# A norm's modulation on ScalarE or VectorE by a rule, and masked copies behind a condition

## Chip, cores and metric

One of the eight cores of a Trainium2 chip runs the whole kernel in one launch. The metric is the device time of that launch in microseconds. The core has five engines with a queue of their own each: TensorE (PE in the profile; its weight loads are PEld), VectorE (DVE), ScalarE (ACT), GpSimd (POOL) and SyncE (SP), which issues most of the loads.

## What is computed

Two layers over 128 context tokens (b = 0) and 128 latent tokens (b = 1), model width 2048, fp32. Layer 0 is attention, layer 1 a bidirectional state-space mixer (S5); each is followed by a gated MLP with a width-3 convolution (FFN). Each of the four sub-layers starts with a norm and a modulation:

```
h  = rms_norm(x, g) * (1 + scale) + shift          # per channel, from c_ctx or c
x += gate * sublayer(h)
# S5, per direction, 128 groups of 16 channels, 64 complex states:
u   = h @ w_in
s_t = abar * s_{t-1} + B u_t                       # scan over the tokens
y   = gelu(d*u + Re(C s)) ; out = (y * sigmoid(y @ w_gate)) @ w_out
```

A final norm gives y_prompt and y_sample; keys, values and the last scan states are outputs too.

## The kernel before

Each weight unit (128 x 1024 numbers, 512 KB) is loaded into one of eight raw buffers and split for the matmuls: ScalarE rounds it to a high part (whi), VectorE subtracts to get the low part (wlo). There are three whi/wlo buffers, so splits run up to two units ahead. Activations are split in the same way. A product is the sum of three matmuls (high x high, low x high, high x low) into PSUM.

The program is written out by a planner in Python that runs while the kernel is built. `Timeline` holds a clock for each engine (`tl.t`), and every emitted instruction moves its engine's clock by an estimated cost, after what it reads is ready by the same estimate. Side work (norm parameters, attention, FFN's convolution, the S5 scan) is held in generators; `pump()`, called after each weight unit, lets a generator go on when its condition holds by these clocks. `written(ap, lag=...)` is such a condition: the estimated time at which `ap` is written has been passed by TensorE's clock, and neither ScalarE nor VectorE is more than `lag` ahead of it. The order of emission is the order in each engine's queue; on the chip each engine works its queue in that order and waits on semaphores.

`Norm.make` makes the input of one group of k-tiles (four tiles of 128 channels, two in the first two groups of layer 0) for one b. `scale_rows` has VectorE multiply rows of x by 1/rms ahead of time. Then TensorE transposes the tiles into one PSUM bank (`tr`), the modulation multiplies by scale and adds shift per partition, one instruction per tile, ScalarE rounds the result to the high part, VectorE subtracts for the low part. For b = 0 the modulation is on ScalarE, for b = 1 on VectorE. There are ten makes in layer 0's first norm and eight in each of the other three. In the first up block of FFN 0 and FFN 1 and the first block of S5's w_in, three units are computed for b = 0 first and then for b = 1.

S5 works in four quarters q of 512 channels. `w_in` for a quarter ends with two transposes on VectorE that write u(q) and then sets `u_ready[q]`. `scan_task` waits for that flag, copies u(q) twice on ScalarE with a mask per parity (um), has TensorE multiply um by tables (T), and ScalarE writes the products into SC(q). `steps_task` runs the 32 scan steps of a quarter on VectorE, four instructions each. `out_task` copies the states out on ScalarE and has TensorE make y(q), which w_gate then reads. In the trace u, um, h and the split activations are named A, SC is X or S.

All instructions of ScalarE, VectorE and GpSimd, and the DMAs, stand on line 302, matmuls on 404, transposes on 417.

Of the kernel before, what the change touches and what calls it, by code (L numbers as in the profile page):

```python
# [29 lines left out]
S5_LAG = 20  # L30
# [8 lines left out]
Y_TAGS = ('A8', 'A8', 'A2', 'S0')  # L39
GATE_SPLIT = (2, 3)  # L40
SCAN_LAG = 5
TAIL_SPLIT = 1
HEAD_FIRST = 1
T_TAGS = ("A3", "A5", "A3", "A12", "A3", "A8", "A3", "A8")
# [3 lines left out]
def view(t, off, dims, parts=None):  # L48
    p0, pn = (0, t.shape[0]) if parts is None else parts
    ps = t.ap[0][0]  # L50
    return bass.AP(tensor=t.tensor, offset=t.offset + p0 * ps + off,
                   ap=[[ps, pn]] + [list(d) for d in dims])
# [292 lines left out]
def hybrid_kernel(ctx: ExitStack, tc: tile.TileContext, a):  # L345
# [7 lines left out]
    tl = Timeline()  # L353
    TL.append(tl)

    def sb(tag, shape, dt=FT, bufs=1):
        count[0] += 1
        t = pool.tile(list(shape), dt, tag=tag, name=f"{tag}_{count[0]}", bufs=bufs)
        tl.place(t, tag, bufs)
        return t  # L360
# [12 lines left out]
    def ms():  # L373
        return ps("ms", [P, 512], 3)
# [4 lines left out]
    def written(*aps, lag=LAG, ahead=0.1):  # L379

        t = tl.ready(*aps)
        return lambda now: max(t - ahead, tl.t["ACT"] - lag, tl.t["DVE"] - lag) < now

    def ready(*aps, lag=LAG, ahead=0.1):

        t = tl.ready(*aps)
        return lambda now: max(max(t, tl.free("ms", 3)) - ahead, tl.t["ACT"] - lag, tl.t["DVE"] - lag) < now
# [14 lines left out]
    def mm(out, lhsT, rhs, **kw):  # L402
        tl.matmul(out, lhsT, rhs, "tile_position" in kw)
        nc.tensor.matmul(out, lhsT, rhs, **kw)  # L404
# [9 lines left out]
    def tr(out, in_):  # L414
        n = in_.shape[0]
        tl.matmul(out, in_, ident, transpose=True)
        nc.tensor.transpose(out, in_, ident[:n, :n])  # L417
# [211 lines left out]
    def block(w, r0, nkt, n0, ncol, xof, done, head=False, tail=False):  # L629
# [11 lines left out]
        def part(bs, kt0, n, hi, lo):  # L641
            rest = []
            last = kt0 + n == nkt
            for b in bs:
                for kk in range(n):
                    xt, k = xof(kt0 + kk, b)
                    products(cell["acc"], b, xt, k, hi, lo, kk, ncol, kt0 + kk == 0, rest)
            remaining(rest, last, (lambda b: done(cell["acc"], b)) if last else lambda b: None)

        for c0 in range(0, nkt, 4):  # L650
            nk = min(4, nkt - c0)

            def run(k0, n, hi, lo, c0=c0):
# [14 lines left out]
                for i, u in enumerate(cell["kept"] + [me]):  # L668
                    part((1,), *u)
                    if skew == 2 and (head or TAIL_SPLIT <= i < 2):  # L670
                        state["cap"] += 1
# [83 lines left out]
    def ada_need(l, part, kt0, nt=4):  # L755
        for k in range(nt):
            wait_for(ada_tasks[l, part, kt0 + k])
# [24 lines left out]
    class Norm:  # L782
# [25 lines left out]
        def make(self):  # L808
            if self.made == len(self.cells):
                return  # L810
            g, b = self.cells[self.made]
            kt0, nt = self.groups[g]
            l, n = self.l, self.n
            self.scale_rows()
            ada_need(l, 3 * n, kt0, nt)
            ada_need(l, 3 * n + 1, kt0, nt)
            if g not in self.tiles:
                self.tiles[g] = sb(self.tags[g], [P, 2, nt, 256], FR)
            t = self.tiles[g]
            h = self.tmp[0][:, self.made % 4]  # L820
            xn = self.tmp[1][:, self.made % 4, :nt * P]
            ps = ms()
            for k in range(nt):
                tr(ps[:, k * P:(k + 1) * P], xn[:, k * P:(k + 1) * P])
            c = slice(b * P, (b + 1) * P)
            for k in range(nt):
                kt = kt0 + k
                src, dst = ps[:, k * P:(k + 1) * P], h[:, k]
                if self.perm:
                    src = src.rearrange("p (c j) -> p j c", j=4)  # L830
                    dst = dst.rearrange("p (j c) -> p j c", j=4)
                s1, s0 = scale[n][:, kt, b:b + 1], shift[n][:, kt, b:b + 1]
                if b == 0:
                    act(dst, src, AF.Identity, bias=s0, scale=s1)
                else:
                    dve.tensor_scalar(dst, src, s1, s0, op0=OP.mult, op1=OP.add)
            act(t[:, 0, :, c], h[:, :nt], AF.Copy)
            dve.tensor_sub(t[:, 1, :, c], h[:, :nt], t[:, 0, :, c])
            self.made += 1
            self.scale_rows()  # L840
            if self.made == len(self.cells):
                norms.remove(self)
# [683 lines left out]
    class S5:  # L1526
# [64 lines left out]
        def scan_task(self):  # L1591
            while not self.u_ready[0]:
                yield
            wt = self.wt = sb("A11", [P, 2048])
            self.kt = sb("A10", [P, 2048])
            w1 = view(wt, 0, [[64, 2], [32, 2], [1, 32]])
            w2 = view(wt, 128, [[64, 2], [32, 2], [1, 32]])
            for q in range(4):
                while not self.u_ready[q]:
                    yield  # L1600
                while q > 1 and not self.sc_free[q - 2] or q == 1 and not prep[0].done:
                    yield
                um = sb("A2", [P, 16, 2, 2, 32])
                SC = self.SC[q] = sb(("X", "S0")[q % 2], [P, 33, 2, 2, 32])
                u = self.u(q).rearrange("p (r n) -> p r n", n=64)
                for par in range(2):
                    act(um[:, :, par].rearrange("p r b c -> p r (b c)"), u, AF.Copy, scale=mask_par[:, par:par + 1])
                dve.memset(SC[:, 0, :, 0], 0.0)
                dve.tensor_copy(SC[:, 0, :, 1], s5par["H0"][:, :, 32 * q:32 * q + 32])
                for e2 in range(2):  # L1610
                    e = 2 * q + e2
                    while e not in self.tT:
                        yield
                    tT = self.tT[e]
                    for h in range(2):
                        for ri in range(2):
                            yield ready(um, tT[:, h], lag=S5_LAG, ahead=AHEAD)
                            bk = ms()
                            for i in range(4):
                                pr = e2 * 8 + h * 4 + i  # L1620
                                mm(bk[:, i * P:(i + 1) * P], tT[:, h, i, ri],
                                   um[:, pr].rearrange("p a b c -> p (a b c)"), start=True, stop=True)
                            src = bk.rearrange("p (g b c) -> p c b g", b=2, c=32)
                            g0 = e2 * 16 + h * 8
                            fw = view(SC, 128 + ri * 64 + g0, [[128, 32], [32, 2], [1, 8]], (0, 64))
                            bw = view(SC, 32 * 128 + ri * 64 + g0, [[-128, 32], [32, 2], [1, 8]], (64, 64))
                            act(fw, src[0:64], AF.Copy)
                            act(bw, src[64:128], AF.Copy)
                    self.t_used[e] = True
                while self.scanned < q - 1:  # L1630
                    yield
                a_re = view(s5par["A4"], 32 * q, [[0, 2], [0, 2], [1, 32]])
                a_im = view(s5par["A4"], G + 32 * q, [[G, 2], [0, 2], [1, 32]])
                yield written(SC, lag=S5_LAG, ahead=AHEAD)
                self.scans.append((SC, a_re, a_im, w1, w2, q))

        def steps_task(self):
            q = 0
            while q < 4:
# [3 lines left out]
                for s in range(32):  # L1643
# [6 lines left out]
                    dve.tensor_tensor(nxt, nxt, w1, OP.add)  # L1650
                    yield lambda now: tl.t["DVE"] < now + SCAN_LAG
                self.scanned = q
# [316 lines left out]
```

## Time and profile before

| | |
|---|---|
| median of three runs | 2554.88 us (2553.78 to 2556.22) |
| the profiled execution | 2553.2 us, its span 2551.4 us |
| mean granted TensorE clock | 0.993 of full speed |
| TensorE busy | 2481.2 us, 97% |
| VectorE busy | 1669.7 us, 65% |
| ScalarE busy | 1285.4 us, 50% |
| GpSimd busy | 473.1 us, 19% |
| DMA, mean over the span | 256 GB/s |

The span runs from the first to the last instruction of one execution. Busy shares are averages over stages; what an engine waited for stands in brackets behind an instruction, as idle time and releaser. The stages follow each other: layer 0's norm and q, k, v up to about 390 us, attention's output to 520, FFN 0 to 1355, S5 to 1790, FFN 1 to the end.

### The profile page before, as it was taken

Reading aid. Unit: us, or ns where it says so; the run is one execution under the profiler, and the core shown is the slowest. Engines: PE = TensorE matmul, PEld = TensorE weight load, DVE = VectorE, ACT = ScalarE, POOL = GpSimd, SP = SyncE. Lnnn points to the kernel's source line nnn. Section 1 sums busy time; section 2 is a strip of 40 time slices with the busy share of each in tenths; the row PEclk is TensorE's granted clock in tenths of the full one; section 3 lists DMA queues with packets and bytes.
Section 4 is the critical chain, followed back from the end, with each engine's and each line's share of the span. In section 5 each row is a group of like instructions: output and inputs, shape, how many; then the busy total and the mean of one; then the engine's idle time right before and its main releaser. Section 6 shows DMA issues by size and latency. Waiting matters only on the chain. (4 is left out here: it accounts for less than half of the span.)

```text
span 2551.4 us, 37505 instructions
## 1 busy us (share of the span) xinstructions
PE 2481.2 (97%) x13883; PEld 1939.1 (76%) x13883; DVE 1669.7 (65%) x2575; ACT 1285.4 (50%) x1900; POOL 473.1 (19%) x493
## 2 busy tenths in 40 slices
PE   7999999999999999999999989999999999999998
PEld 5676776668887887788776766767688888888886
DVE  3655564578686676676666788454666665766576
ACT  5333354465664564555455554444555544554454
POOL 0002000013565555555511011000000000000000
PEclk9999999999999999999999999999999999999999
DMA  9879978978988888888779677789687766666663
GB/s 359 318 268 295 319 237 301 337 266 258 274 286 264 276 256 261 275 264 271 264 255 322 235 247 246 252 292 317 225 256 242 239 197 185 190 188 196 188 202 124
DMA packets 460495, 653.61 MB, mean 256 GB/s; under 512 B 65420, under 2 KB 245772, under 8 KB 457368
## 3 DMA queue, kind: packets, MB, share of 16 engines
q1 hardware_dynamic: 451744, 620.32, 74.4%
q0 software_dynamic: 8208, 30.35, 3.6%
q8 instruction: 109, 1.79, 0.3%
q14 instruction: 74, 0.61, 0.1%
q10 hardware_dynamic: 360, 0.55, 0.1%
HBM read 623.72 MB, written 27.39 MB: 255 GB/s over the span
## 5 line engine op out<-in xcount | busy, mean ns | idle before, releaser
L302 DVE TENSOR_TENSOR wlo<-raw,whi 128x1024 fp32r<-128x1024 f32 (+1 forms) x694 | 895.2, 1295 | 613.1 <-ACT whi L302 604.8
L302 ACT ACTIVATE whi<-raw 128x1024 fp32r<-128x1024 f32 (+1 forms) x694 | 728.9, 1054 | 597.7 <-PE acc L404 353.4
L404 PE MATMUL acc<-whi,A 128*128 128x512 f32 x3040 | 788.8, 399 | 28.8 <-ACT whi L302 15.4
L404 PEld LDWEIGHTS acc<-whi,A 128*128 128x128 f32 x3040 | 563.2, 189 | 198.3 <-ACT whi L302 33.7
L404 PE MATMUL acc<-A,whi 128*128 128x512 f32 x2496 | 674.2, 395 | 0.0
L404 PEld LDWEIGHTS acc<-A,whi 128*128 128x128 f32 x2496 | 429.9, 189 | 78.4 <-issue 12.2
L404 PE MATMUL acc<-wlo,A 128*128 128x512 f32 x1520 | 415.9, 393 | 0.7 <-DVE wlo L302 0.7
L404 PEld LDWEIGHTS acc<-A,wlo 128*128 128x128 f32 x2496 | 372.3, 190 | 45.7
L404 PE MATMUL acc<-A,wlo 128*128 128x256 f32 x2496 | 383.4, 281 | 0.0
L404 PEld LDWEIGHTS acc<-wlo,A 128*128 128x128 f32 x1520 | 286.8, 189 | 65.2 <-DVE wlo L302 2.4
L302 POOL TENSOR_TENSOR S<-S,A 128x512 f32<-128x512 f32 x128 | 181.7, 1439 | 50.4 <-PE ms L417 50.4
L404 PE MATMUL ada<-raw,cond 128*32 128x512 f32 (+1 forms) x1408 | 169.4, 592 | 1.5 <-DMA raw<-in_ada_w_dram 1.5
L302 POOL DMA_DIRECT2D adab<-in_ada_b_dram x48 | 24.8, 516 | 727.2 <-DVE ada L302 372.6
L302 DVE SCALAR_TENSOR_TENSOR A<-acc,cw,A 128x254 f32<-128x254 f32 x312 | 142.4, 477 | 6.2 <-ACT A L302 0.7
L302 POOL TENSOR_TENSOR S<-S 128x512 f32<-128x512 f32 (+1 forms) x96 | 138.3, 1440 | 7.5
L302 ACT ACTIVATE A<-A 128x512 fp32r<-128x512 f32 (+4 forms) x127 | 81.1, 641 | 113.6 <-DVE A L302 112.5
L302 ACT ACTIVATE A<-acc 128x256 f32<-128x256 f32 (+1 forms) x188 | 69.1, 420 | 110.2 <-PE acc L404 110.1
L302 DVE TENSOR_TENSOR acc<-acc,A 128x256 f32<-128x256 f32 (+1 forms) x228 | 108.9, 508 | 23.6 <-PE acc L404 22.4
L404 PEld LDWEIGHTS ms<-A,A 128*64 128x64 f32 (+1 forms) x1152 | 86.8, 193 | 20.5 <-ACT A L302 8.4
L302 ACT ACTIVATE A<-ms 128x512 f32<-128x512 f32 (+3 forms) x106 | 55.8, 558 | 88.6 <-PE ms L404 69.1
L404 PEld LDWEIGHTS ada<-raw,cond 128*32 128x32 f32 x1408 | 37.9, 109 | 81.3 <-issue 69.8
L404 PE MATMUL ms<-A,A 128*64 128x64 f32 (+1 forms) x1152 | 90.3, 271 | 9.6 <-ACT A L302 5.8
(149 smaller groups left out, 1670.5 us busy)
## 6 DMA issues: line engine op xcount, KB each, us to landing
raw<-in_ada_w_dram SPq DMA_DIRECT2D x334, 512.0 KB
raw<-in_ffn_w_up_dram SPq DMA_DIRECT2D x334, 512.0 KB
raw<-in_ffn_w_down_dram SPq DMA_DIRECT2D x168, 512.0 KB
raw<-in_na_w_qkv_dram SPq DMA_DIRECT2D x68, 512.0 KB
raw<-in_s_w_in_dram SPq DMA_DIRECT2D x32, 512.0 KB
raw<-in_s_w_gate_dram SPq DMA_DIRECT2D x32, 512.0 KB
raw<-in_s_w_out_dram SPq DMA_DIRECT2D x32, 512.0 KB
A<-in_na_w_qkv_dram SPq DMA_DIRECT2D x28, 512.0 KB
```

Source lines behind the costliest of these rows:

```text
L302: return fn(*args, **kw)
L404: nc.tensor.matmul(out, lhsT, rhs, **kw)
```

## The change

A make asks the planner's clocks, once the transposes are emitted, which engine could begin first. If ScalarE, or TensorE where that is later, plus 0.5 us is no later than VectorE, or TensorE where that is later, all of the make's modulations go to ScalarE, otherwise to VectorE; b no longer matters. In `scan_task` the two masked copies are emitted when `written(u, lag=20)` holds instead of as soon as the generator gets there; the memset and the copy of the start state on VectorE follow them, as before.

```diff
+MOD_ACT = 1
...
             c = slice(b * P, (b + 1) * P)
+            by_act = max(tl.t["ACT"], tl.t["PE"]) + 0.5 * MOD_ACT <= max(tl.t["DVE"], tl.t["PE"])
             for k in range(nt):
...
-                if b == 0:
+                if by_act:
                     act(dst, src, AF.Identity, bias=s0, scale=s1)
                 else:
                     dve.tensor_scalar(dst, src, s1, s0, op0=OP.mult, op1=OP.add)
...
                 u = self.u(q).rearrange("p (r n) -> p r n", n=64)
+                yield written(u, lag=S5_LAG)
                 for par in range(2):
                     act(um[:, :, par].rearrange("p r b c -> p r (b c)"), u, AF.Copy, scale=mask_par[:, par:par + 1])
```

## Rows read from the trace of the kernel before

**Rows 1.** The page: busy time, share of the span and instructions of each engine.

```profile
PE 2481.2 (97%) x13883; PEld 1939.1 (76%) x13883; DVE 1669.7 (65%) x2575; ACT 1285.4 (50%) x1900; POOL 473.1 (19%) x493
```

**Rows 2.** TensorE's waits: what it waited for, us in total, times, longest.

```profile
PE acc L404 <- ACT whi L302: 15.4, 9, 3.4
...
PE acc L404 <- ACT A L302: 11.8, 12, 2.4
...
PE ms L417 <- DVE A L302: 7.3, 5, 1.9
```

**Rows 3.** Groups by shape on ScalarE and VectorE: count, busy us, mean ns, idle before.

```profile
L302 ACT ACTIVATE A<-ms,shift,scale 128x128 f32<-128x128 f32 x64 | 24.0, 453 | 21.9 <-PE ms L417 17.0 <-DVE scale L302 5.0
...
L302 DVE TENSOR_SCALAR A<-ms,scale,shift 128x128 f32<-128x128 f32 x64 | 21.8, 401 | 0.0
```

**Rows 4.** Timeline near 114 us: start, us, what, count, idle before and its releaser.

```profile
111.54 0.60 PE L417 MATMUL ms<-ident,A 128*128 128x128 f32 x4
...
114.53 1.36 DVE L302 TENSOR_SCALAR A<-ms,scale,shift 128x128 f32<-128x128 f32 x4
...
115.92 0.63 ACT L302 ACTIVATE A<-A 128x512 fp32r<-128x512 f32 x1 [3.81 <-DVE A L302]
...
116.60 1.00 PE L404 MATMUL acc<-whi,A 128*128 128x512 f32 x2 [2.43 <-ACT A L302]
...
121.98 1.08 PE L404 MATMUL acc<-wlo,A 128*128 128x512 f32 x4
```

**Rows 5.** Timeline near 69 us.

```profile
69.31 0.42 ACT L302 ACTIVATE A<-A 128x256 fp32r<-128x256 f32 x1 [1.93 <-DVE A L302]
...
69.78 0.73 PE L404 MATMUL acc<-whi,A 128*128 128x512 f32 x2 [1.69 <-ACT A L302]
```

**Rows 6.** Timeline of the first makes of FFN 0.

```profile
525.41 1.50 ACT L302 ACTIVATE A<-ms,shift,scale 128x128 f32<-128x128 f32 x4 [0.82 <-PE ms L417]
...
533.15 0.60 PE L417 MATMUL ms<-ident,A 128*128 128x128 f32 x4
...
535.89 0.63 ACT L302 ACTIVATE A<-A 128x512 fp32r<-128x512 f32 x1 [3.13 <-DVE A L302]
...
536.57 0.50 PE L404 MATMUL acc<-whi,A 128*128 128x512 f32 x1 [1.16 <-ACT A L302]
...
545.21 0.63 ACT L302 ACTIVATE A<-A 128x512 fp32r<-128x512 f32 x1 [2.62 <-DVE A L302]
...
545.23 0.66 PE L417 MATMUL ms<-ident,A 128*128 128x128 f32 x4 [1.85 <-DVE A L302]
```

**Rows 7.** Timeline around the masked copies of quarters 0 and 1.

```profile
1396.19 2.19 ACT L302 ACTIVATE A<-A,maskpar 128x1024 f32<-128x1024 f32 x2 [3.47 <-DVE A L302]
...
1430.76 1.30 DVE L302 STREAM_TRANSPOSE A<-acc 128x512 f32<-128x512 f32 x2
...
1432.10 2.19 ACT L302 ACTIVATE A<-A,maskpar 128x1024 f32<-128x1024 f32 x2 [8.30 <-DVE A L302]
...
1435.26 3.50 DVE L302 TENSOR_TENSOR wlo<-raw,whi 128x1024 fp32r<-128x1024 f32 x3 [3.07 <-ACT whi L302]
...
1435.28 3.78 PE L404 MATMUL acc<-whi,A 128*128 128x512 f32 x8 [3.19 <-ACT whi L302]
```

**Rows 8.** Timeline, one undisturbed unit's eight matmuls.

```profile
1408.56 2.09 PE L404 MATMUL acc<-whi,A 128*128 128x512 f32 x8
```

**Rows 9.** Timeline before and after the end of scan 1.

```profile
1483.93 1.23 DVE L302 TENSOR_TENSOR wlo<-raw,whi 128x1024 fp32r<-128x1024 f32 x1 [5.21 <-ACT whi L302]
...
1522.87 8.55 ACT L302 ACTIVATE A<-S 64x1024 f32<-64x1024 f32 x8
...
1525.03 0.50 PE L404 MATMUL ms<-A,A 128*64 128x64 f32 x2 [4.19 <-ACT A L302]
```

**Rows 10.** Stretch: us, busy of PE, PEld, DVE, ACT, POOL, clock, DMA share, GB/s.

```profile
1436.00:1438.00 2.00, 2.00 (x6) 1.52 (x5) 2.00 (x3) 1.12 (x2) 0.00 (x0) 0.50 0.20 31
```

**Rows 11.** Chain that ended last: start, us, what.

```profile
1679.81 10.25 DMA raw<-in_s_w_out_dram
```

## The prediction

> **What bounds the kernel now.** I read the page first: TensorE is busy 2481 of 2551 us [rows 1], so a change can only win what TensorE idles, some 70 us, and the time in which it runs at the lower clock. The list of TensorE's waits then says who holds it: 15.4 us for split copies of weights on ScalarE, 11.8 us for activations written by ScalarE, 7.3 us for ones written by VectorE [rows 2]. These few entries are where both edits act. The groups by shape give the two prices of one modulation, 453 ns on ScalarE and 401 ns on VectorE, 64 of each today [rows 3]: 17 makes with b = 0 go to ScalarE, 17 with b = 1 to VectorE. Last I read the timeline around every stretch in which TensorE stops near a make or near the S5 scan [rows 4 to 11].
>
> **Part one, the modulation.** It removes and adds no instruction; it moves groups of two or four between two engines that each take their work in order. Four take 1.50 us on ScalarE [rows 6] and 1.36 us on VectorE [rows 4], so with both engines free a move to ScalarE costs 0.14 us and the other way gains it. What can be worth more is the work queued in front. In the b = 1 makes VectorE stands behind splits and adds while ScalarE, which must do the next step (the rounded copy), sits idle.
>
> The make near 114 us: the transposes end at 111.54 + 0.60 = 112.14. VectorE starts the modulation at 114.53. ScalarE's copy starts at 115.92 after 3.81 us idle, so it was free from 112.11; TensorE has waited 2.43 us when it goes on at 116.60 [rows 4]. On ScalarE: start 112.2 (0.1 us after the transposes, as elsewhere), plus 1.50, plus the copy 0.63, makes 114.35, 2.2 us earlier. The matmuls behind the stop are slow too: 116.60 to 121.98 is 5.38 us for 16 of them, where eight take 2.09 us in an undisturbed unit [rows 4, 8], so 16 want 4.18: another 1.2 us. Term: 3.4 us.
>
> The make near 69 us (two tiles): ScalarE was free at 69.31 - 1.93 = 67.38 and TensorE waited 1.69 us [rows 5]. Two modulations at about 0.8 and a copy of 0.42 end at 68.65 instead of 69.73. Term: 1.1 us. A like stop of 1.1 us at 25.9 us is left out; loads are tight there.
>
> In each of three norms (FFN 0, S5, FFN 1) the same pair of stops comes twice; I show FFN 0. At 536.57 TensorE has waited 1.16 us: transposes end at 533.75, ScalarE was free from 535.89 - 3.13 = 532.76; on ScalarE the modulation would end at 533.85 + 1.50 = 535.35 instead of 535.86, 0.5 us. At 545.23 TensorE has waited 1.85 us: ScalarE was free at 545.21 - 2.62 = 542.59, would end at 544.1 instead of 545.17, 1.1 us [rows 6]. Three norms: 4.8 us.
>
> Sum of part one: 3.4 + 1.1 + 4.8 = 9.3 us, if the rule picks ScalarE at all these places. It looks at the program's own clocks, which I can't see in a trace; by the queues VectorE is over 1 us behind ScalarE at most of them and about 0.7 us behind the transposes at the three of 0.5 us [rows 4 to 6]. I take seven tenths, 6.5 us, since some picks will fall the other way. Lower end 0; upper end everything and the stop at 25.9 us too: 10.4. The makes near 187 and 273 us have no stop of TensorE beside them and are costed at nothing; the cover is the split copies already made for two units, and without it a make would cost its 1.50 us.
>
> VectorE's own page of the Trainium skill (VectorE: DVE Perf Modes, Specifications) says that ScalarE sits closer to PSUM, by which a modulation that reads PSUM would be quicker there. The trace differs: 453 against 401 ns, 1.50 against 1.36 us for four [rows 3, 4, 6]. The skill's ScalarE: Activation LUTs (What ACT_TABLE_LOAD costs) adds about 93 ns for each per-partition operand, and this instruction has two; that speaks against the move, in the trace's direction. By the first page the sum would be some tenths more, by the second it stays as it is.
>
> **Part two, the masked copies.** It moves two ScalarE instructions of some 1.1 us in each of four quarters behind a condition; SP's and POOL's queues get nothing new. For quarters 2 and 3 the input has been there long before, no effect. For quarter 0 ScalarE idles 3.47 us in front of them but TensorE runs through [rows 7], nothing to win; the price, if the copies and so the products behind them slip by one unit of 12 matmuls, is 2.7 us of a later scan.
>
> Quarter 1 is the place. ScalarE waits 8.30 us at the head of its queue, from 1423.8 to 1432.10, for two transposes that VectorE, busy with scan steps, starts only at 1430.76. Queued behind are the splits of the next units; so VectorE idles 3.07 us (1432.2 to 1435.26) and TensorE 3.19 us (to 1435.28), and its eight matmuls then take 3.78 us, against 2.09 [rows 7, 8]; the granted clock there is 0.50, the lower of its two levels [rows 10]. With the copies emitted a unit or two later the splits pass in front and TensorE saves 3.2 + 1.7 = 4.9 us at this place.
>
> It does not keep them. At 1525.03 TensorE has waited 4.19 us for copies that ScalarE starts at 1522.87, when scan 1 on VectorE has ended [rows 9]. The two scans run back to back on VectorE up to there, so the end moves only by what VectorE gains: its 3.07 us. I take 3.1 us. Lower end -2.7 (quarter 0 slips and VectorE's idle turns up again elsewhere: it stood 5.21 us for a split at 1483.93 [rows 9]); upper end 4.9.
>
> **Sum.** 6.5 + 3.1 = 9.6 us off the profiled 2553.2 us (span 2551.4 and 1.8 around it) is 2543.6. The median of the three runs is 1.7 above the profiled one, so I say 2544.
>
> **Rivals.** (A) The rule seldom fires where TensorE stops, and only part two is left: 2553.2 - 3.1 = 2550. For it: the rule ties to VectorE, and its margin of 0.5 us is as large as the smaller stops. Against it: the idle of ScalarE before the copies is 1.9 to 3.8 us.
>
> (B) TensorE arrives earlier and waits elsewhere: the load that the chain of waits shows at 1679.81 for 10.25 us [rows 11], or the scan. For it: weights are read nearly all the time. Against it: those loads are issued when earlier buffers come free, so they move along. If all of part one before FFN 1 is given back and the scan term too, 1.6 x 0.7 = 1.1 us remains: 2552.
>
> (C) Slower. The rule's tie goes to VectorE, so b = 0 makes leave ScalarE wherever the program believes VectorE free within 0.5 us. Where VectorE in truth runs behind that belief, as at quarter 1, whose transposes start 7 us after ScalarE began to wait for them [rows 7], each such make pays what the b = 1 makes pay now. If b = 0 makes inherit the whole 9.3 us and b = 1 makes keep theirs, less 3.1 of part two, the time is 2559; it decides from a lag of VectorE of over 0.5 us behind the program's clock at the b = 0 makes. Against it: at those makes VectorE has splits and adds queued, which the program counts.
>
> (D) The schedule is redrawn: with other engine clocks the program emits fillers and background steps elsewhere, a few us either way. It widens the range and has no time of its own.
>
> **Chances.** Forecast 0.62 (own range 2537 to 2549), A 0.13, B 0.13, C 0.12. The range, 2536 to 2555, takes in A, B and the upper ends (10.4 + 4.9 off is 2538), and leaves out C and tails. About 0.2% (5.1 us) is what a measurement of this kernel can tell from no change. Faster by more: the forecast nearly whole and a piece of A and B, 0.68; within: the rest of those, 0.20; slower: 0.12.
>
> **What would show it.** Right: the groups by shape count more than 64 modulations on ScalarE, fewer on VectorE; no stop of TensorE over 1 us near 116, and under 1 us for the pairs in the three norms; ScalarE's 8.30 us wait gone and no lower clock near 1436; the wait before the first copies after scan 1 longer than 4.19 us, its end some 3 us nearer to the stage's start. Wrong: modulations on ScalarE falling below 64, TensorE's waits for split copies growing past 15.4 us, or scan 1 ending no earlier against the end of the first quarter's matmuls.

## The result, and the profile after

The changed kernel takes 2532.83 us (median of four runs, 2532.28 to 2533.63) against 2554.88 before: ratio 0.9914, 95% interval 0.9897 to 0.9931. Run again beside later experiments it took 2533.54 us, ratio 0.9920 (0.9904 to 0.9937). The forecast was 2544 and its range ended at 2536: the direction was right, the gain, 22 us, is twice the forecast one. The two profiled executions differ by 20.1 us of span (2551.4 and 2531.3), and the sums below account for those. In the changed kernel all line numbers are one higher.

The page's line of engines and, below it, TensorE's waits (us in total, times, longest) and the modulations by shape, all of the kernel after:

```profile
PE 2477.4 (98%) x13883; PEld 1936.5 (77%) x13883; DVE 1656.6 (65%) x2525; ACT 1303.2 (51%) x1950; POOL 477.3 (19%) x493
```

```profile
PE acc L405 <- ACT whi L303: 13.1, 8, 3.5
...
PE ms L405 <- ACT A L303: 7.1, 3, 4.9
PE acc L405 <- ACT A L303: 4.2, 9, 1.6
```

```profile
L303 ACT ACTIVATE A<-ms,shift,scale 128x128 f32<-128x128 f32 x114 | 42.7, 452 | 9.6 <-PE ms L418 4.7 <-DVE scale L303 3.3 <-PE acc L405 1.7
...
L303 DVE TENSOR_SCALAR A<-ms,scale,shift 128x128 f32<-128x128 f32 x14 | 4.8, 403 | 5.6 <-PE ms L418 5.5
```

114 of 128 modulations are on ScalarE (64 before [rows 3]). TensorE's waits for activations from ScalarE fell from 11.8 to 4.2 us, those of its transposes for VectorE, 7.3 us before [rows 2], to 0.8.

Where the 20.1 us went follows from the same landmark in both traces (the same transpose, split or state copy), as start before minus start after:

| stretch (us, before) | gain | forecast term |
|---|---|---|
| layer 0's norm, up to 140 | 7.4 | 4.5 |
| attention and its loads, 140 to 524.72 | -0.7 | 0 |
| FFN 0's norm, 524.72 to 549.95 | 2.5 | 1.6 |
| rest of FFN 0 | -0.1 | 0 |
| S5's norm, 1357.86 to 1389.48 and what leads to it | 1.4 | 1.6 |
| S5, quarters 0 and 1, to scan 0's end at 1472.20 | 6.0 | 3.1 |
| rest of S5 | -0.5 | 0 |
| FFN 1's norm, 1790.76 to 1822.34 | 3.8 | 1.6 |
| rest of FFN 1 | 0.3 | 0 |

The terms of part one, 9.3 us in all, were then cut to seven tenths.

### The profile page after: what moved, and what is told of

It is laid out like the page before. It is cut to its first block, busy times and chain, and to the rows that moved or that the text cites. A ratio compares the mean times of both kernels' runs of the same rounds, so it can differ in the third digit from the quotient of the medians.

```text
span 2531.3 us, 37512 instructions
## 1 busy us (share of the span) xinstructions
PE 2477.4 (98%) x13883; PEld 1936.5 (77%) x13883; DVE 1656.6 (65%) x2525; ACT 1303.2 (51%) x1950; POOL 477.3 (19%) x493
## 4 chain that ended last, share of the span: by engine, by line
PE 89%; DMA 4%; ACT 3%; DVE 3%; POOL 1%; issue 1%; SPq 0%; ACTq 0%; POOLq 0%; DVEq 0%
PE acc L405 76%; PE ada L405 6%; PE ms L405 4%; PE ms L418 2%; ACT A L303 1%; POOL S L303 1%; DVE A L303 1%; DMA raw<-in_na_w_o_dram 1%; ACT whi L303 1%; DMA raw<-in_s_w_in_dram 1%; DMA raw<-in_ada_w_dram 1%; DMA raw<-in_na_w_qkv_dram 1%; DVE S L303 1%; DVE wlo L303 0%; DMA A<-in_ffn_w_up_dram 0%
```

## Experiments

Theory T: the two parts add up, and each stop of TensorE that they touch goes whole. Each ratio is to the kernel before, run on the same chip, with its 95% interval.

| kernel | us, median (lowest to highest) | ratio |
|---|---|---|
| rule alone | 2538.82 (2536.01 to 2541.49) | 0.9943 (0.9931 to 0.9956) |
| condition alone | 2549.91 (2545.64 to 2551.56) | 0.9984 (0.9975 to 0.9992) |
| condition, quarter 1 alone | 2548.21 (2546.89 to 2552.69) | 0.9979 (0.9970 to 0.9988) |
| all on ScalarE | 2535.78 (2532.07 to 2537.62) | 0.9928 (0.9916 to 0.9941) |
| b swapped | 2549.89 (2544.28 to 2551.26) | 0.9980 (0.9970 to 0.9989) |
| VectorE filler, planner told | 2536.60 (2534.41 to 2538.30) | 0.9933 (0.9918 to 0.9947) |
| TensorE filler, planner told | 2542.46 (2535.61 to 2543.24) | 0.9950 (0.9935 to 0.9965) |
| VectorE filler, not told | 2538.72 (2537.59 to 2541.96) | 0.9939 (0.9924 to 0.9954) |
| TensorE filler, not told | 2536.20 (2534.58 to 2540.94) | 0.9930 (0.9916 to 0.9945) |
| both engines modulate | 2573.59 (2568.78 to 2575.90) | 1.0071 (1.0056 to 1.0086) |
| VectorE's old load | 2537.04 (2535.38 to 2538.55) | 0.9928 (0.9914 to 0.9943) |
| state copies, quarter 0 | 2527.38 (2525.15 to 2528.83) | 0.9897 (0.9881 to 0.9914) |
| the same and last states | 2527.27 (2523.83 to 2529.00) | 0.9889 (0.9874 to 0.9903) |
| state copies, all quarters | 2552.26 (2546.15 to 2555.37) | 0.9989 (0.9979 to 0.9999) |

Ten of the traces have the same code up to attention's end, and yet ScalarE's 127th split of weights starts there at 502.8 to 508.0 us (mean 504.5); in the kernel before and the two with its norms it starts at 508.8 to 511.9 us (mean 510.3). So layer 0 keeps some 5.8 us of its gain, while attention's loads scatter by 5 us. A median therefore settles no question of 2 us here; the stretches of the traces do.

**The parts apart.** The rule alone (the condition's line taken out), the condition alone (`by_act` back to `b == 0`), and the condition for one quarter:

```diff
-                yield written(u, lag=S5_LAG)
+                if q == 1:
+                    yield written(u, lag=S5_LAG)
```

> The rule for the modulation alone; the masked copies are emitted as before the change. The two traces together place 14.2 us of the gain of 20.1 us ahead of FFN 0's end, in S5's norm and in FFN 1's norm, and 5.9 us in the stretch between the transposes of quarter 1 and the end of scan 0. Theory T (the parts stand apart, and each stop in a norm goes whole): this kernel takes 13 to 15 us off the kernel before, 2540 to 2542 us, and its trace still has the wait of about 8 us of ScalarE before the masked copies of quarter 1 and VectorE's two idle stretches of about 3 us each behind it. Rival R1 (the scan stage was shortened because the norm ahead of it left the engines in another order, so that the rule gives nearly all): at most 2536 us, with scan 0 ending some 16 us earlier than before.

> The condition ahead of the masked copies alone, for every quarter; the modulation goes by b as before the change. Theory T (VectorE's second idle stretch, 2.83 us at 1446.74 in the kernel before, was a consequence of the first of 3.07 us at 1435.26, so both go): 5.5 to 6.5 us less than the kernel before, about 2549 us, with all of it between the transposes of quarter 1 and the end of scan 0. The prediction's term for this part, kept as a rival (only the first stretch goes): 3 us, about 2552 us. Rival R1 (the rule gives nearly all): within 1 us of the kernel before.

> The condition ahead of the masked copies for quarter 1 alone, and the modulation by b as before the change. Theory T: only quarter 1's copies had anything queued behind them that was due, so this equals the kernel with the condition for all four quarters, about 2549 us, within 1 us. Rival: quarter 0's copies (3.47 us idle before them on ScalarE) or those of quarters 2 and 3 carry a part: 1 to 3 us slower than with all four.

The rule alone gives 14.4 us, as T has it. Its trace still shows ScalarE's wait of 8.30 us and VectorE's first idle stretch of 3.07, but the second, 2.83 us, which I expected to stay, is gone; that miss is taken up below. The condition alone shortens the stretch up to scan 0's end by 6.0 us, for quarter 1 alone by 5.9: quarter 0 carries nothing, as forecast. The medians show 3.3 and 5.0, below T's 5.5 to 6.5, and their intervals don't tell them apart; in these two traces 1.7 and 3.0 us had been lost ahead of S5, where the code is the same. R1 is out by its own signs: the rule alone stays above 2536 us, and its trace keeps the 8.30 us wait. The gains of the medians, 14.4 + 3.3 to 5.0, fall 1.5 to 4.4 us short of the 20.9 and 22.1 measured together, which at this scatter says little. Within the stretch up to scan 0's end they don't add up as T has it: the rule alone shortens it by 2.7 us (82.72 to 80.00), the condition alone by 6.0, and both together by 6.0. So beside the rule the condition is worth 3.3 us there.

**Which makes go where.**

```diff
-            by_act = max(tl.t["ACT"], tl.t["PE"]) + 0.5 * MOD_ACT <= max(tl.t["DVE"], tl.t["PE"])
+            by_act = True        # all on ScalarE; in the other kernel: b == 1
```

> The changed kernel with all 128 modulations on ScalarE instead of 114. Theory T (what helps is that ScalarE is free when a make's transposes end and that VectorE is spared 1.36 us per make; the choice by the clocks adds little): within 2 us of the changed kernel, 2531 to 2535 us. Rival R3 (the choice itself matters, the 14 modulations left on VectorE stand where ScalarE is behind): slower than the changed kernel by 2 to 4 us, about 1 us for each of the makes moved.

> The changed kernel with the modulation of b = 0 on VectorE and that of b = 1 on ScalarE, 64 each: the numbers of the kernel before, the other way round; the condition ahead of the masked copies stays. Theory T (each engine's own delay counts: a make of either b behind a busy VectorE stops TensorE): like the kernel with the condition alone, the stops return at the makes of b = 0, and the time lies 10 us or more above the changed kernel. Rival R4 (only b = 1 was ill placed, because its make follows that of b = 0 and VectorE was late there): at most 5 us above the changed kernel.

All on ScalarE isn't told apart from the changed kernel by its ratio (0.9928 against 0.9920), but its median lies 2.2 to 3.0 us above, outside T's 2 us and where R3 put it. The traces speak against R3: beside the changed kernel's first trace one norm is longer by 0.8 us (layer 0), one by 0.6 (S5), FFN 0's is 1.2 shorter, FFN 1's is equal. The choice by clocks earns nothing that is shown here. With b = 0 on VectorE the whole gain of the rule is lost, and stops are back at 25.37 (2.76 us) and at 534.95 (2.94 us). R4 is out; rival C of the prediction had the right mechanism for makes of b = 0 that stand behind VectorE, at a price that was too low (9.3 us; the swap costs 16), but the rule sent only 14 of those 64 modulations there.

**Is it the order, or VectorE's time?** First VectorE repeats each modulation of b = 1 from the same PSUM bank; then, in its place, it does two multiplications from its own rows.

```diff
                     act(dst, src, AF.Identity, bias=s0, scale=s1)
+                    if b == 1:                      # first kernel
+                        nc.vector.tensor_scalar(t[:, 1, k, c], src, s1, s0, op0=OP.mult, op1=OP.add)
...
+            if by_act and b == 1:                   # second kernel
+                for _ in range(2):
+                    nc.vector.tensor_tensor(t[:, 1, :, c], rows, rows, OP.mult)   # rows: xn, as the tile is laid out
             act(t[:, 0, :, c], h[:, :nt], AF.Copy)
```

> The changed kernel in which VectorE also does each of the 64 modulations of b = 1, into a place that its later subtraction overwrites, without telling the planner: every other instruction keeps its order. ScalarE still makes the values that are used, so VectorE is as loaded as in the kernel before but no longer in the path of the rounded copy. Theory T2 (a stop goes whole because VectorE is also spared 1.36 us in each of these makes): 4 us or more of the gain of part one is lost, and stops of 1 us and more return in the norms of FFN 0 and FFN 1. Rival R7 (only the order counts: the modulation no longer waits behind VectorE's queue): within 2 us of the changed kernel, with the stops still gone.

> The changed kernel in which VectorE does two multiplications of 128x512 more (0.69 us each) in each make of b = 1, from the rows that it scaled itself into a place that its later subtraction overwrites, without telling the planner: VectorE is as loaded as in the kernel before and has no part in the path of the rounded copy, and the PSUM bank is read by ScalarE alone. Theory T2 (a stop goes whole because VectorE is also spared 1.36 us): 4 us or more of the gain of part one is lost, and stops of over 1 us return in the norms of FFN 0 and FFN 1. Rival R7 (only the order counts): within 2 us of the changed kernel, stops still gone.

The first is 40 us slower, which fits T2 by the number alone: it did not test what it was made for. The timeline of its FFN 0 shows why: the two engines take turns at the bank, tile by tile.

```profile
542.18 0.41 DVE L838 TENSOR_SCALAR A<-ms,scale,shift 128x128 fp32r<-128x128 f32 x1
...
542.62 0.46 ACT L303 ACTIVATE A<-ms,shift,scale 128x128 f32<-128x128 f32 x1 [1.74 <-DVE A L838]
...
543.11 0.41 DVE L838 TENSOR_SCALAR A<-ms,scale,shift 128x128 fp32r<-128x128 f32 x1 [0.53 <-ACT A L303]
...
543.56 0.46 ACT L303 ACTIVATE A<-ms,shift,scale 128x128 f32<-128x128 f32 x1 [0.48 <-DVE A L838]
```

So VectorE is in the path again, and ScalarE's modulations start 0.94 us apart, where alone four take 1.50 us [rows 6]. The Trainium skill (PSUM — Partial Sum Buffer, PSUM bank collisions raise a hardware error) says that the compiler's scheduler makes any two instructions of different engines on one bank and quadrant wait for each other, reads too; the waits here agree. One thing the run does tell: all 64 modulations of b = 1 were on ScalarE, since only those are repeated, and 64 were.

The second kernel answers. VectorE carries its old load again (34 multiplications, 22.3 us), and in FFN 0's norm TensorE shows only this (its waits there, without a stop of 0.5 us):

```profile
529.71 0.73 PE L405 MATMUL acc<-whi,A 128*128 128x512 f32 x2 [0.16 <-DVE A L303]
...
532.23 0.73 PE L405 MATMUL acc<-whi,A 128*128 128x512 f32 x2 [0.41 <-DVE A L303]
```

T2's stops of over 1 us don't return there or in FFN 1's norm (the longest is 0.63 us). The median is 3.5 us above the changed kernel's second set, though, beyond R7's 2 us. Of the 4.1 us between the two traces 3.6 arise ahead of FFN 0: 1.3 in layer 0's norm, the rest in attention's loads, which scatter by more. FFN 0's norm is 0.8 us shorter than in the second run, S5's 0.4 and FFN 1's 0.8 longer. So R7 holds in the main: what counts is that the modulation no longer waits in VectorE's queue. VectorE's freed time is worth some 2 us more by these norms, only in part beyond the scatter.

**What sets S5's quarters 0 and 1.** Fillers on either engine, first through the planner (four memsets; 24 products into a bank that nothing reads):

> The changed kernel with four memsets of 128x768 more on VectorE after step 20 of scan 0, on a part of a buffer that is not yet in use; nothing computed changes. Estimated at 2.9 us of VectorE's time together, the price of the first idle stretch that went (3.07 us at 1435.26). Theory T (VectorE's queue sets the end of scan 0 and scan 1, so that a stretch of VectorE's time is worth itself): the end of scan 0 and TensorE's restart after scan 1 come later by the memsets' time, within 0.7 us, and the time grows by 2 to 3 us. Rival R2 (the stage was shortened on TensorE's side, by the stop of 3.19 us at 1435.28 and the lower clock behind it): scan 0's end may move, but the time grows by under 1 us.

> The changed kernel with 24 matmuls more on TensorE in the third part of quarter 1's table products, into PSUM that nothing reads; nothing computed changes. 24 such matmuls take 2.5 to 2.9 us. Theory T (in this stage TensorE has slack that ends in the stop of 4.86 us before the first copies after scan 1): the stop shrinks by about the matmuls' time and the time grows by under 0.7 us. Rival R2 (TensorE is the bound there): the time grows by 2.5 to 2.9 us and the stop stays near 4.9 us.

Both are inconclusive. Told of the extra time, the planner emitted other work elsewhere: with VectorE's filler the end of scan 0 came 4.6 us later but TensorE's restart after scan 1 only 0.5; with TensorE's the trace behind it is 4.7 us longer for some 5.3 us of products (the 2.5 to 2.9 us expected were too few: each of these fp32 products stands in the trace as two matmuls). So both were repeated with instructions that the planner doesn't see, every other one keeping its place:

```diff
+                    if q == 0 and s == 20:
+                        for _ in range(4):
+                            nc.vector.memset(view(self.wt, 1280, [[1, 768]]), 0.0)
```

```diff
                                 mm(bk[:, i * P:(i + 1) * P], tT[:, h, i, ri],
                                    um[:, pr].rearrange("p a b c -> p (a b c)"), start=True, stop=True)
+                                if e == 2 or e == 3 and h == 0:
+                                    # the same product once more, by nc.tensor.matmul
```

> The changed kernel once more, as the measure for the three kernels beside it. 2531 to 2535 us.

> The changed kernel with the same four memsets on VectorE after step 20 of scan 0 (3.47 us from first to last in the earlier run), now without telling the planner: every other instruction stands in the changed kernel's order. Theory T (VectorE's queue sets the ends of scan 0 and scan 1): both come 3 to 3.5 us later and TensorE's stop of 4.86 us before the first copies after scan 1 grows by as much, the time by 2.5 to 3.5 us. Rival R2 (TensorE and its clock set the stage): under 1 us. Rival R6 (VectorE's idle 5.20 us in scan 1 takes it up, since it waits there for ScalarE): scan 0's end 3.5 us later and scan 1's end less than 1 us later.

> The changed kernel with 24 table products of quarter 1 on TensorE done twice into the same place, without telling the planner: every other instruction stands in the changed kernel's order. The extra products take 2.5 to 2.9 us. Theory T: the stop of 4.86 us before the first copies after scan 1 shrinks by 2 to 2.9 us and the time grows by under 1 us. Rival R2 (TensorE is the bound up to there): the stop stays and the time grows by 2.5 us or more.

The 24 products of TensorE's filler are 48 matmuls in the trace and take 5.1 us, twice what was expected (1422.26 to 1435.71 for the stretch that holds them, 13.45 us, against 8.23 without). Compared from the same split ahead of both fillers, VectorE's 3.5 us put scan 0's end 3.4 us later, and TensorE's 5.1 us put it 3.9 us later; at the end of the trace 2.6 and 3.0 us remain. The medians lie 5.2 and 2.7 us above the second set; the scatter allows that. So both engines count here: VectorE's time in full up to scan 0's end, of TensorE's about three quarters; where the other 1.2 us were taken up was not followed. R6 is out (the idle stretch in scan 1, 5.21 us, is as long as before), and so is each single-bound theory: TensorE alone as the bound would have cost all 5.1 us, and T's forecast for TensorE's filler (under 1 us, the stop after scan 1 shrinking) fails too. How VectorE's delay reaches TensorE stands in TensorE's waits with VectorE's filler:

```profile
1446.61 1.21 PE L405 MATMUL acc<-wlo,A 128*128 128x512 f32 x4 [1.18 <-DVE wlo L303]
...
1450.79 1.21 PE L405 MATMUL acc<-wlo,A 128*128 128x512 f32 x4 [1.12 <-DVE wlo L303]
...
1513.12 0.45 PE L405 MATMUL ms<-A,A 128*64 128x64 f32 x2 [4.27 <-ACT A L303]
```

The weights' low parts stand between the scan steps in VectorE's queue, so a late scan step makes TensorE wait for wlo. The other way round VectorE waits with TensorE's filler, where without it the first wait is 0.26 us and the second is none:

```profile
1430.13 1.23 DVE L303 TENSOR_TENSOR wlo<-raw,whi 128x1024 fp32r<-128x1024 f32 x1 [2.06 <-ACT whi L303]
...
1442.81 1.23 DVE L303 TENSOR_TENSOR wlo<-raw,whi 128x1024 fp32r<-128x1024 f32 x1 [1.12 <-ACT whi L303]
```

It waits for splits on ScalarE, which stand there behind copies of TensorE's products. The stop before the first copies after scan 1, which T let grow or shrink, stays (4.12 us without fillers, 4.30 with TensorE's).

**A version with more of the same.** Three splits still stood behind eight state copies on ScalarE (8.55 us), and VectorE waited 5.20 us for one of them at 1467.47.

```diff
                     for h in range(2):
+                        if q == 0:
+                            yield written(SC, lag=4, ahead=AHEAD)
```

The other two add the same condition ahead of the small copy of the last states, and drop `if q == 0`.

> A version after the same idea: the changed kernel with a condition ahead of each two of the eight copies of quarter 0's states that stand as one stretch of 8.55 us on ScalarE at 1457.81 with a weight split behind them; they then follow the next three splits. VectorE waits 5.20 us for that split at 1467.47, in the middle of scan 1. Theory T (VectorE's queue sets scan 1's end, and an idle stretch goes whole): scan 1 ends 4 to 6 us earlier, and the time falls by 3 to 5 us, as far as TensorE's stop of 4.86 us before the first copies after scan 1 reaches. Rival R5 (the copies are themselves due: the products that read them and the third quarter's tables, which need their buffer, come later): no gain or up to 3 us slower.

> The version with quarter 0's state copies behind a condition, and a condition also ahead of the small copy of each quarter's last state, which waits 7.65 us at the head of ScalarE's queue at 1455.75 with two splits behind it. Theory T (a stage in which TensorE is full gains what TensorE idles): TensorE's stop of 0.58 us there and VectorE's of 1.27 us go, 0.5 to 1.5 us less than the version with the state copies alone. Rival: the order of emission shifts elsewhere and it is slower by up to 3 us.

> The version with the condition ahead of each two state copies for all four quarters instead of quarter 0 alone. Theory T: the later quarters' copies stand where TensorE waits for them (the 4.86 us stop is such a wait), so putting them back gains nothing: within 1 us of the version for quarter 0, or slower. Rival: another 1 to 3 us.

For quarter 0 alone it takes 2527.38 us. All its four runs lie below all eight of the changed kernel, 6.2 us below the median of the second set. VectorE's 5.20 us are gone, and TensorE meets the next quarter's products with a stop of 2.31 us and one of 0.32, in place of the stops of 0.95, 2.20, 4.12 and 1.64 us that the changed kernel's second run has there: 6.3 us less, which is what the trace gains between scan 0's end and FFN 1. That is more than T's 3 to 5 us, and R5 is out. ScalarE's stretch of that trace shows the copies behind the splits:

```profile
1454.27 2.94 ACT L303 ACTIVATE whi<-raw 128x1024 fp32r<-128x1024 f32 x3
1457.52 1.06 ACT L303 ACTIVATE whi<-raw 128x1024 fp32r<-128x1024 f32 x1 [0.30 <-DVE S L303]
1462.36 1.06 ACT L303 ACTIVATE whi<-raw 128x1024 fp32r<-128x1024 f32 x1 [3.77 <-PE acc L405]
1463.32 8.57 ACT L303 ACTIVATE A<-X 64x1024 f32<-64x1024 f32 x8
```

The small copy adds nothing that can be told apart (2527.27). For all quarters it is 25 us worse: T had the sign, but no size; TensorE stops 15.32 us at 1614.34 until VectorE has written an activation, and that chain was not followed further.

## Why the prediction was right in kind and wrong in size

**Part one, the stops in the norms: the step that failed is the pairing.** I took the modulation at 534.50 to read the transposes at 533.15 [rows 6], and so let it start on ScalarE no earlier than 533.85: 0.5 us of a stop of 1.16. It reads transposes one make earlier. The timeline before, with the rows that I had not shown:

```profile
531.28 0.60 PE L417 MATMUL ms<-ident,A 128*128 128x128 f32 x4
...
532.12 0.63 ACT L302 ACTIVATE A<-A 128x512 fp32r<-128x512 f32 x1
...
538.97 0.60 PE L417 MATMUL ms<-ident,A 128*128 128x128 f32 x4
...
543.81 1.36 DVE L302 TENSOR_SCALAR A<-ms,scale,shift 128x128 f32<-128x128 f32 x4
```

Counted in order, the makes' transposes are at 524.72, 529.22, 531.28, 533.15, 536.91, 538.97, and their modulations at 525.41, 530.61, 534.50, 537.55, 539.49, 543.81: the third belongs to 531.28, the sixth to 538.97. The third could start on ScalarE at 532.76, end at 534.3 and be rounded by 534.9, before TensorE stopped at 535.41 (536.57 - 1.16): the stop goes whole. The same makes after, where the third modulation starts before the fourth make's transposes do:

```profile
524.88 0.63 PE L418 MATMUL ms<-ident,A 128*128 128x128 f32 x4
...
527.12 1.49 ACT L303 ACTIVATE A<-ms,shift,scale 128x128 f32<-128x128 f32 x4
...
527.61 0.60 PE L418 MATMUL ms<-ident,A 128*128 128x128 f32 x4
...
528.64 0.63 ACT L303 ACTIVATE A<-A 128x512 fp32r<-128x512 f32 x1
...
531.98 0.60 PE L418 MATMUL ms<-ident,A 128*128 128x128 f32 x4
...
534.25 1.49 ACT L303 ACTIVATE A<-ms,shift,scale 128x128 f32<-128x128 f32 x4
```

The sixth starts 1.7 us after its transposes instead of 4.2, and the 1.85 us stop of 545.23, which I let shrink by 1.1, is gone too. So a norm's pair of stops, 3.0 us, goes whole; how much of it is kept differs, 2.5 us in FFN 0 and less in S5. FFN 1 shows the most, 3.8 us: beside 3.1 us of idle time, 0.7 us of TensorE's busy time went (window, time, TensorE's busy time; before, then after):

```profile
1790.76:1822.34 31.58, 26.64 (x140) 17.34 (x141) 24.09 (x49) 18.23 (x34) 0.50 (x1) 1.00 0.49 167
...
1774.76:1802.57 27.81, 25.97 (x140) 17.56 (x140) 20.15 (x34) 24.99 (x51) 0.51 (x1) 1.00 0.57 189
```

In S5's norm the pair is gone as well, yet only 1.4 us are kept: TensorE, earlier now, meets a load. This is rival B in small.

```profile
1370.12 1.06 ACT L303 ACTIVATE whi<-raw 128x1024 fp32r<-128x1024 f32 x1 [4.12 <-DMA raw<-in_s_w_in_dram]
...
1371.23 2.11 PE L405 MATMUL acc<-whi,A 128*128 128x512 f32 x8 [0.89 <-ACT whi L303]
...
1376.00 2.11 PE L405 MATMUL acc<-whi,A 128*128 128x512 f32 x8 [1.75 <-ACT whi L303]
```

**Layer 0.** The makes near 69 and 114 us gave 1.3 and 3.8 us, against terms of 1.1 and 3.4. The stop at 25.9 us, left out because "loads are tight there", gave about 2.3, of which 1.3 is faster work (TensorE's granted clock up to 66.78 us was 0.92 before and 0.96 after): the loads did not take it back before 140 us. In this pair of traces 0.7 of the whole 7.4 is given back later, by the mean of the ten 1.6. At 114 us the gain is 2.2 us of idle time and 1.6 of faster work, where I had 1.2 (granted clock 0.91 before, 1.00 after).

**The cut to seven tenths** (2.8 us) was a doubt about picks without a row behind it. The rule put all 64 modulations of b = 1 on ScalarE. Rival A and rival C needed the opposite. The choice between the engines' own prices mattered as little as said: 452 and 403 ns now. The Trainium skill (VectorE: DVE Perf Modes, Specifications) has ScalarE closer to PSUM; no gain from that shows here, and the trace decides.

**Part two: "It does not keep them" failed.** The place, the 8.30 us wait and its end were right; after, the copies start at 1422.09 without any wait. I took VectorE's chain of scan steps as the bound and so only its first idle stretch, 3.07 us, as gain, with 4.9 as the upper end. But VectorE's own account was short too: further on it idles a second time in the same stretch, in a row of the kernel before that I had not counted, and 3.07 + 2.83 is nearly the 6.0 that went:

```profile
1446.74 1.23 DVE L302 TENSOR_TENSOR wlo<-raw,whi 128x1024 fp32r<-128x1024 f32 x1 [2.83 <-ACT whi L302]
```

And TensorE counts as well. In the same stretch, before and then after (time, TensorE's busy time, and the granted clock third from the end):

```profile
1389.48:1472.20 82.72, 79.50 (x414) 64.54 (x415) 59.96 (x161) 43.58 (x56) 6.07 (x12) 0.96 0.74 242
```

```profile
1379.01:1455.75 76.74, 76.70 (x414) 62.43 (x415) 59.64 (x161) 43.96 (x56) 6.08 (x12) 1.00 0.80 267
```

TensorE is full after. What went is its 3.2 us of idle time and 2.8 us of slower work (79.50 - 76.70), 6.0 in all, and nothing of it came back by the end of scan 1. The 1.7 us that I had for slow matmuls were for eight of them; it was more. The rule alone parts the two: it has the same stop, 3.19 us, without the lower clock. The 17 matmuls around the stop, in the kernel before and in that one:

```profile
1430.89:1440.57 9.68, 6.48 (x17) 4.80 (x18) 6.51 (x15) 5.03 (x5) 0.00 (x0) 0.68 0.46 142
```

```profile
1420.14:1427.40 7.26, 4.07 (x17) 3.03 (x17) 4.19 (x7) 5.03 (x5) 0.00 (x0) 1.00 0.29 85
```

The granted clock was 0.68 in one (part of it at 1.2 GHz, [rows 10]) and 1.00, 2.4 GHz, in the other: 2.4 us. VectorE's second idle stretch, 2.83 us, is gone there too, so I take it for a result of TensorE's slow matmuls and no delay of its own; that rests on one trace of each kernel. It also means that against a kernel without the lower clock the condition is worth the 3.3 us found above, near the forecast 3.1, and that the rest hangs on the clock. Of the three signs that I named for this part, the wait's end and the clock came true, and the wait before the first copies after scan 1 grew (4.19 to 4.86 us), but by 0.7 instead of 3 us, because TensorE's earlier arrival was matched by the scan's.

**In sum.** The forecast took 9.6 us off the profiled execution, the traces show 20.1. Of the 10.5 us between them 2.8 are the cut, 2.9 the three norms (7.7 against 4.8), 2.9 layer 0 (7.4 against 4.5) and 2.9 the S5 stage, less 1.0 given back elsewhere. The times of the two profiled executions lie 19.6 us apart; the medians lie 22.1 apart, because that of before was 1.7 us below its median and that of after 0.8 above. Rival D, the redrawn schedule, stayed small here: outside the stretches named, the two traces differ by about 1 us in sum.

**Left open.** Whether the lower clock near 1436 is in every execution of the kernel before is not shown; there is one profile of it, and two kernels without its cause show medians 3.3 and 5.0 us lower. Why attention's loads scatter by 5 us between traces was not tried.

## What to carry to other kernels

Before a stop is priced, pair each producer with its consumer by counting them through the stage, not by which stands next in time: queues that run a step ahead make the nearest row the wrong one. An instruction that waits at the head of an engine's queue costs what stands behind it, so look for idle time whose releaser is another engine's busy queue, and move either the instruction or its emission; here that paid three times, gave nothing measurable once, and failed once where the moved work was itself due. Where two engines wait for each other's work, neither alone is the bound: price a stop by both, its lower clock included. Here VectorE's extra time counted in full at the end of the scan, TensorE's to three quarters.

## What the runs showed of the hardware

A like stop of 3.19 us on TensorE was followed by matmuls at a mean granted clock of 0.68 in one kernel and at 1.00 in another (9.68 and 7.26 us for 17, one trace each); which it was is worth 2.4 us. Two engines that were to read one PSUM bank took turns tile by tile, so that ScalarE's modulations started 0.94 us apart (542.62 to 543.56), where four take 1.5 us alone. One 128x128 product of fp32 tables stands in the trace as two matmuls: 24 of them added 48, and 5.1 us.
